# A two-layer streaming trunk: token-range tiles at the end of a mixer, FFN operands in two stages, an earlier first group of the second product, a bias table in three parts

## The chip, the cores and the metric

The kernel runs on one core of a Trainium2 chip. The metric is the device time of one execution in microseconds, as the median of several runs. The text calls the engines by their short names in the profile: PE is the tensor engine, PEld its weight loads, DVE is VectorE, ACT is ScalarE, POOL is GpSimd, and SP is the queue that issues nearly all transfers.

## The reference

One inference step of a trunk of two layers, on 1024 prompt tokens and 32 sample tokens (T = 1056), with 1024 features, in fp32. Layer 0 mixes by a gated linear recurrence, layer 1 by differential attention with a relative-position bias table. Each layer then ends in the same way, and this end is what the change touches:

```
x = x + rmsnorm(mixer(rmsnorm(x)), g_post)                  # sandwich norm
h = rmsnorm(x, g_in)
g, u = split(h @ w_ffn_in)                                  # 1024 -> 2 x 2816
g = causal depthwise conv of width 3 over tokens(g) + bias
f = (silu(g) * u) @ w_ffn_out                               # 2816 -> 1024
x = x + rmsnorm(f, g_post2)
x = x + sigmoid(x @ w_ple_gate) * (p @ w_ple)               # gated per-layer input
```

The bias of a head for a query and a key depends on their distance alone: `rel_bias[bucket(rel)]`, with 32 buckets and 8 heads.

## The kernel before

Features lie on partitions and tokens along the columns. An fp32 product is made of three matmuls of fp32r operands: each operand is split into a high part (a cast on ACT, L167 or L108) and a low part (a subtraction on DVE, L168 or L109), and `mm3` (L118 to L120) issues high x high, high x low and low x high. Tokens are cut in three groups GT: 384, 384 and 288 columns (t = 0, 1, 2).

`layer_end` is called once per layer. First `mixer_out` adds the second half of the mixer's output product: units (t, j) for three token groups and eight feature blocks j. In units of t = 0 the first half's result is added on DVE; in units of t = 1 and 2 an identity matmul adds it in PSUM (L292) and ACT copies it out (L293). `sumsq` squares on ACT (L200) and sums on POOL (L201) into `acc[t]`. `norm_m(t)` normalises, adds the residual (L308, L309), stores to `xm` and sums squares into `xacc[t]`; `norm_x(t)` (L318) writes the FFN's input y, eight tiles of 1060 columns. After the units, `ple` makes the per-layer input's product in eight steps, with norm_m(2) issued at step 0, norm_x(1) at step 1 and norm_x(2) at step 5. The matmul over `ones` in `rstd_ps` (L188) sums over partitions. PE's order there is the one written in the code.

The FFN's first product is done by seven products of half size instead of eight: the tokens are cut in two halves of HT = 528 columns and the features in two halves, `operands` makes the token-side operands b1 to b7 (differences of y, L398 to L401, then splits), `weights7` the weight-side ones, and `ffn_in` does 22 factors ft, one for each 128 of the 2816 hidden features. Each factor ends in the convolution and the gate (L499 to L504) and stores a row of 1056 columns to `hd`.

`ffn_out` makes the second product in groups of two or three hidden rows: each row is read from `hd`, split, and its weights `wfo` are loaded as a `piece` (L103, L108, L109). Group 0 is copied into f by ACT (L552), later groups are added on DVE (L554). The last group runs by token group; `post(t)` (L528, L529) norms the result, followed by the gates. Before group 3 of layer 0, `bias_table` loads the 0/1 table of buckets (`onehot`) in a raw slot, multiplies it with `rel_bias`, and stores the result to `bd`, which one transfer of 4608 KB then repeats over 128 partitions into `zd`.

A scheduler orders the instructions of each engine by program order, readiness and priority (`tc.high_priority()` raises it). Pools hand out tiles by tag: a tile waits until the slot's last user is done. `raw` has two slots of 1152 columns, shared by all weight loads. SP takes its transfers in order, and one that waits holds back those behind it.

Of the kernel before, what the change touches and what calls it, by code (L numbers as in the profile page):

```python
# [18 lines left out]
P = 128  # L19
# [19 lines left out]
HT = T // 2  # L39
NEG = -3.0e38  # L40
# [4 lines left out]
class Trunk:  # L45
# [228 lines left out]
    def mixer_out(self, l, wsrc, gpost, resid, fp):  # L274

        nc, tc, io = self.nc, self.tc, self.io
        with tc.tile_pool(name=self.nm("mo"), bufs=1, reuse_waits="tile") as mp:
            acc = [mp.tile([P, n], F32, tag=f"acc{t}", name=self.nm("acc")) for t, (_, n) in enumerate(GT)]
            xacc = self.new_acc()
            w = [self.piece(wsrc[1, jp]) for jp in range(4)]  # L280
            self.og_load(self.og, 4, 3, [2])
            ple = self.ple_load(l, mp)
            y = [fp.tile([P, T + 4], F32, tag="y", name=self.nm("y"), bufs=8) for _ in range(KD)]
            g_in = self.G(4 * l + 2)

            def unit(t, j):


                ps = self.half_unit(w, self.og, j, 4, t, t == 0)
                m = self.m[j][t].bitcast(F32)  # L290
                if t:
                    nc.tensor.matmul(ps, self.ident, m, start=False, stop=True)  # L292
                    nc.scalar.copy(m, ps)  # L293
                else:
                    nc.vector.tensor_tensor(m, ps, m, ADD)
                self.sumsq(acc[t], m, j == 0, mp)

            rm, rx = [None] * 3, [None] * 3

            def norm_m(t):  # L300
                self.ln_exp()
                rm[t] = self.rstd_ps(acc[t], D)
                t0, n = GT[t]
                for j in range(KD):
                    m = self.m[j][t].bitcast(F32)
                    x0 = mp.tile([P, 384], F32, tag="x0", name=self.nm("x0"), bufs=4)[:, :n]
                    nc.sync.dma_start(x0, resid[j][:, t0:t0 + n])
                    nc.vector.scalar_tensor_tensor(m, m, gpost[:, j:j + 1], rm[t], MUL, MUL)  # L308
                    nc.vector.tensor_tensor(m, m, x0, ADD)  # L309
                    nc.sync.dma_start(self.xm[j][:, t0:t0 + n], m)  # L310
                    self.sumsq(xacc[t], m, j == 0, mp)

            def norm_x(t):
                rx[t] = self.rstd_ps(xacc[t], D)
                t0, n = GT[t]
                for j in range(KD):
                    m = self.m[j][t].bitcast(F32)
                    nc.vector.scalar_tensor_tensor(y[j][:, t0:t0 + n], m, g_in[:, j:j + 1], rx[t], MUL, MUL)  # L318
# [17 lines left out]
        return y  # L336
# [12 lines left out]
    def ple(self, pool, ple, wpl):  # L349

        nc = self.nc
        for j in range(KD):
            js = slice(j * P, (j + 1) * P)
            pe = pool.tile([P, T], F32, tag="pe", name=self.nm("pe"), bufs=2)
            for t, (t0, n) in enumerate(GT):
# [3 lines left out]
                nc.scalar.copy(pe[:, t0:t0 + n], ps)  # L359
# [7 lines left out]
    def layer_end(self, l, wsrc, gpost, resid, last):  # L367

        tc = self.tc
        with self.phase("ff", 1, 2, m=4, r=1) as fp:  # L370
            y = self.mixer_out(l, wsrc, gpost, resid, fp)
            self.xp.release()
            op = self.right("op", 1)
            self.ffn_in(l, self.operands(y, op), fp)
            op.release()
            self.xp = self.right("xp", 16)
            with tc.tile_pool(name=self.nm("fo"), bufs=1, reuse_waits="tile") as f2:
                self.ffn_out(l, fp, f2, last)

    def operands(self, y, op):  # L380
# [3 lines left out]
        for p in (7, 5, 4, 1, 2, 3, 6):  # L384
            out[p] = [[op.tile([P, HT], F32R, tag=f"b{p}{k}{i}", name=self.nm(f"b{p}")) for i in range(2)]
                      for k in range(4)]

        def put(p, kh, hf):
            for k in range(4):
                self.split(b[kh][hf][k], *out[p][k])  # L390

        b = [[[y[4 * kh + k][:, HT * hf:HT * hf + HT] for k in range(4)] for hf in range(2)] for kh in range(2)]
        put(1, 0, 0)
        put(2, 1, 0)
        put(3, 1, 1)
        for k in range(4):
            b11, b12, b21, b22 = b[0][0][k], b[0][1][k], b[1][0][k], b[1][1][k]
            nc.vector.tensor_tensor(b11, b12, b11, SUB)  # L398
            nc.vector.tensor_tensor(b12, b22, b12, SUB)
            nc.vector.tensor_tensor(b22, b22, b11, SUB)  # L400
            nc.vector.tensor_tensor(b21, b21, b22, SUB)  # L401
        put(6, 1, 1)
        put(7, 0, 1)
        put(5, 0, 0)
        put(4, 1, 0)
        return out
# [26 lines left out]
    def ffn_in(self, l, b, fp):  # L433
# [6 lines left out]
        def row(tag="y", n=T + 4, bufs=8):  # L440
            return fp.tile([P, n], F32, tag=tag, name=self.nm(tag), bufs=bufs)

        for ft in range(NFF):
            a = self.weights7(l, ft)
# [14 lines left out]
            p1 = row("p1", HT, 1)  # L459
# [30 lines left out]
            prod(3, Z, more=True)  # L490
            n0, n1 = pieces
# [14 lines left out]
        nc.sync.dma_start(self.io["conv"][l], self.co[l])  # L506

    def ffn_out(self, l, fp, f2, last):
# [23 lines left out]
        groups = [[2 * i, 2 * i + 1] for i in range(8)] + [[16, 17, 18], [19, 20, 21]]  # L532
        for gi, grp in enumerate(groups):
            lastg = gi == len(groups) - 1
            hs, wos = [], []
            for ft in grp:
                raw = f2.tile([P, T], F32, tag="rh", name=self.nm("rh"), bufs=2) if gi else self.raw()[:, 0:T]
                nc.sync.dma_start(raw, self.hd[ft])
                h = [row()[:, 0:T].bitcast(F32R) for _ in range(2)]
                self.split(raw, *h)  # L540
                hs.append(h)
                wos.append(self.piece(io["wfo"][l, ft]))

            def out_unit(j, t):
# [8 lines left out]
                else:  # L553
                    nc.vector.tensor_tensor(f[j][t], ps, f[j][t], ADD)  # L554
                if lastg:
                    self.sumsq(acc[t], f[j][t], j == 0, f2)

            if gi == 3 and not last:
                self.bias_table()
# [457 lines left out]
    def bias_table(self):  # L1017
# [4 lines left out]
        nc.sync.dma_start(oh, io["onehot"])  # L1022
        nc.sync.dma_start(rb, io["rel_bias"])
        for i in range(3):
            ps = self.psm()[0:H, 0:384]
            nc.tensor.matmul(ps, rb, oh[:, i * 384:i * 384 + 384], start=True, stop=True)
            nc.vector.tensor_copy(bt[:, i * 384:i * 384 + 384], ps)
        nc.sync.dma_start(self.bd, bt)
# [294 lines left out]
```

## Time and profile before

| | |
|---|---|
| median of 3 runs | 3063.17 us (3062.08 to 3071.13) |
| the profiled execution, its own time | 3063.09 us |
| its span | 3061.1 us |
| PE busy | 2918.7 us (95%) |
| DVE busy | 1991.8 us (65%) |
| ACT busy | 1307.8 us (43%) |
| POOL busy | 278.5 us (9%) |
| mean granted PE clock | 0.979 |

Busy time is what an engine's instructions take; a share near 100% over a stretch says that the engine sets that stretch's length. The granted clock is PE's own, 1.00 being full speed.

### The profile page before, as it was taken

The numbers are of one execution on the slowest core, as the hardware profiler recorded it, in microseconds if no ns is written. First come the engines' busy times: TensorE is split into PE (matmuls) and PEld (weight loads), VectorE is DVE, ScalarE is ACT, GpSimd is POOL, SyncE is SP. The second block draws the span as 40 slices with busy tenths as digits, with TensorE's granted clock in tenths as the row PEclk, the third lists the DMA queues.
The fourth block names the chain that finished last, engine by engine and source line by source line (L and its number), as shares of the span: only waits on it lengthen the run. The fifth ranks groups of instructions, "written<-read, shape, count | busy, mean of one in ns | idle before, by whom it ended". The sixth has DMA issues, their size and how long they took to land.

```text
span 3061.1 us, 50577 instructions
## 1 busy us (share of the span) xinstructions
PE 2918.7 (95%) x20334; PEld 2800.4 (91%) x20334; DVE 1991.8 (65%) x3786; ACT 1307.8 (43%) x2347; POOL 278.5 (9%) x431
## 2 busy tenths in 40 slices
PE   7999999988999999898999999999889999999989
PEld 7998898978999999898988888989789999999989
DVE  7565555368777765666667575574787777657674
ACT  6444434564433333114445554465643433331151
POOL 0000000140000000002231111001400000000020
PEclk9999999998999999999999999999999999999999
DMA  3111111352222223422332232232512222242242
GB/s 130 38 46 40 45 53 40 104 180 68 72 82 79 79 83 120 158 93 93 124 119 72 85 91 80 90 101 79 181 56 81 74 79 82 81 136 84 84 143 71
DMA packets 104882, 275.32 MB, mean 90 GB/s; under 512 B 12192, under 2 KB 49056, under 8 KB 104648
## 3 DMA queue, kind: packets, MB, share of 16 engines
q1 hardware_dynamic: 102088, 263.71, 25.9%
q0 software_dynamic: 2560, 8.39, 1.3%
q8 instruction: 159, 2.61, 0.3%
q14 instruction: 75, 0.61, 0.1%
HBM read 196.53 MB, written 71.86 MB: 88 GB/s over the span
## 4 chain that ended last, share of the span: by engine, by line
PE 80%; DVE 8%; ACT 6%; DMA 2%; issue 2%; POOL 1%; SPq 0%; POOLq 0%; DVEq 0%; ACTq 0%
PE psm L120 14%; PE psm L119 14%; PE psm L118 13%; PE psd L118 10%; PE psd L119 10%; PE psd L120 10%; PE po L1167 1%; PE pss L1133 1%; PE psm L1159 1%; PE pss L1134 1%; DMA raw<-wfo 1%; POOL xacc L201 1%; ACT sq L200 1%; DVE ws L109 1%; ACT ws L108 1%
## 5 line engine op out<-in xcount | busy, mean ns | idle before, releaser
L118 PE MATMUL psd<-x,ws 128*128 128x384 f32 (+1 forms) x1512 | 519.4, 344 | 9.7 <-ACT x L622 8.8
L119 PE MATMUL psm<-b,ws 128*128 128x264 f32 x1760 | 504.2, 286 | 12.5 <-DVE b L168 12.5
L118 PE MATMUL psm<-b,ws 128*128 128x264 f32 x1760 | 504.0, 287 | 7.7 <-ACT b L167 7.7
L120 PE MATMUL psm<-b,ws 128*128 128x264 f32 x1760 | 504.0, 286 | 0.0
L119 PE MATMUL psd<-x,ws 128*128 128x384 f32 (+1 forms) x1512 | 496.5, 328 | 0.0
L120 PE MATMUL psd<-x,ws 128*128 128x384 f32 (+1 forms) x1512 | 492.0, 325 | 1.3 <-DVE ws L109 1.3
L118 PE MATMUL psm<-y,ws 128*128 128x384 f32 (+1 forms) x1056 | 348.6, 332 | 31.4 <-DVE f L554 14.5
L119 PE MATMUL psm<-y,ws 128*128 128x384 f32 (+1 forms) x1056 | 347.5, 329 | 4.9 <-DVE y L168 4.9
L119 PEld LDWEIGHTS psm<-b,ws 128*128 128x128 f32 x1760 | 335.0, 190 | 13.7 <-DVE b L168 13.7
L120 PE MATMUL psm<-y,ws 128*128 128x384 f32 (+1 forms) x1056 | 346.7, 329 | 0.6 <-DVE ws L109 0.6
L118 PEld LDWEIGHTS psm<-b,ws 128*128 128x128 f32 x1760 | 333.4, 190 | 8.6 <-ACT b L167 8.6
L120 PEld LDWEIGHTS psm<-b,ws 128*128 128x128 f32 x1760 | 334.6, 190 | 0.0
L167 ACT CAST ws<-raw 128x512 fp32r<-128x512 f32 x308 | 190.3, 621 | 325.6 <-DVE raw L429 101.1
L554 DVE TENSOR_TENSOR f<-psm,f 128x384 f32<-128x384 f32 (+1 forms) x432 | 220.6, 521 | 159.8 <-PE psm L120 158.7
L118 PEld LDWEIGHTS psd<-x,ws 128*128 128x128 f32 x1512 | 286.9, 190 | 23.7 <-ACT x L622 9.1
L119 PEld LDWEIGHTS psd<-x,ws 128*128 128x128 f32 x1512 | 287.3, 190 | 8.5 <-issue 0.9
L120 PEld LDWEIGHTS psd<-x,ws 128*128 128x128 f32 x1512 | 286.6, 190 | 6.9 <-issue 3.5
L168 DVE TENSOR_TENSOR ws<-raw,ws 128x512 fp32r<-128x512 f32 x308 | 208.7, 690 | 116.3 <-ACT ws L167 115.8
L109 DVE TENSOR_TENSOR ws<-raw,ws 128x1024 fp32r<-128x1024 f32 (+1 forms) x138 | 168.3, 1221 | 111.6 <-ACT ws L108 111.1
L118 PEld LDWEIGHTS psm<-y,ws 128*128 128x128 f32 x1056 | 203.3, 193 | 35.5 <-DVE f L554 15.1
L119 PEld LDWEIGHTS psm<-y,ws 128*128 128x128 f32 x1056 | 203.9, 193 | 7.6 <-DVE y L168 7.1
L120 PEld LDWEIGHTS psm<-y,ws 128*128 128x128 f32 x1056 | 203.1, 192 | 2.0 <-DVE ws L109 2.0
(295 smaller groups left out, 6083.9 us busy)
## 6 DMA issues: line engine op xcount, KB each, us to landing
raw<-wfi SPq DMA_DIRECT2D x88, 512.0 KB, 3.4
hd<-y SPq DMA_DIRECT2D x44, 528.0 KB, 2.7
raw<-wfo SPq DMA_DIRECT2D x44, 512.0 KB, 4.3
rh<-hd SPq DMA_DIRECT2D x40, 528.0 KB, 3.7
raw<-wia SPq DMA_DIRECT2D x30, 512.0 KB, 3.4
ped<-pe SPq DMA_DIRECT2D x16, 528.0 KB, 2.8
y<-ped SPq DMA_DIRECT2D x16, 528.0 KB, 5.1
raw<-wpg SPq DMA_DIRECT2D x16, 512.0 KB, 3.8
```

What stands on the lines that cost most here:

```text
L108: nc.scalar.copy(wh[:, w], raw[:, w])
L109: nc.vector.tensor_tensor(wl[:, w], raw[:, w], wh[:, w].bitcast(F32), SUB)
L118: mm(ps, wh, xh, start=start and i == 0, stop=False, skip_group_check=more)
L119: mm(ps, wh, xl, start=False, stop=False, skip_group_check=more)
L120: mm(ps, wl, xh, start=False, stop=stop and i == n - 1, skip_group_check=more)
L167: self.nc.scalar.copy(hi, src)
L168: self.nc.vector.tensor_tensor(lo, src, hi.bitcast(F32), SUB)
L200: nc.scalar.activation(sq, src, AF.Square)
L201: (eng or nc.gpsimd).tensor_tensor(acc, acc, sq, ADD)
L554: nc.vector.tensor_tensor(f[j][t], ps, f[j][t], ADD)
L1133: mm(ps[:, :pad], qs[c][:, P * i:P * i + P], kh[c][:, k0:k0 + pad], start=True, stop=False)
L1134: mm(ps[:, :pad], qs[c][:, P * i:P * i + P], kl[c][:, k0:k0 + pad], start=False, stop=True)
```

## The change

The change has five parts. All but the last are done in both layers.

1. `mixer_out` keeps y in three tiles by token range (528, 240 and 288 columns) in a pool of its own. Units of t = 1 are added on DVE instead of PE and ACT; only t = 2 keeps the identity matmul, and its result goes straight to y's third tile. The squares get high priority and those of `xacc` a tag of their own. norm_m(1) is issued after unit (2, 1) instead of (2, 2).
2. `operands` becomes a generator with two stages. The first, begun after norm_x(1) and before norm_x(2), covers b1, b2 and the first 240 columns of the second half; the second does the other 288 columns and the rest. The first factor's weights are split before the second stage.
3. `out_operands`, new, loads and splits a group's rows and weights. For group 0 it is called in the last factor of `ffn_in`, behind product 3.
4. The adds into f and the last squares in `ffn_out` get high priority.
5. `bias_table` works in three parts of 384 columns, in tiles of the tags sg and x0 instead of raw slots.

```diff
@@ mixer_out
-                ps = self.half_unit(w, self.og, j, 4, t, t == 0)
+                ps = self.half_unit(w, self.og, j, 4, t, t < 2)
                 m = self.m[j][t].bitcast(F32)
-                if t:
+                if t == 2:
                     nc.tensor.matmul(ps, self.ident, m, start=False, stop=True)
+                    m = y[j][2]
                     nc.scalar.copy(m, ps)
                 else:
                     nc.vector.tensor_tensor(m, ps, m, ADD)
-                self.sumsq(acc[t], m, j == 0, mp)
+                with tc.high_priority():
+                    self.sumsq(acc[t], m, j == 0, mp)
...
-                    self.sumsq(xacc[t], m, j == 0, mp)
+                    self.sumsq(xacc[t], m, j == 0, mp, tag="sqx")
...
-                    if (t, j) == (2, 2):
+                    if (t, j) == (2, 1):
                         norm_m(1)
                 for j in self.ple(mp, *ple):
                     if j == 0:
                         norm_m(2)
                     if j == 1:
                         norm_x(1)
+                        self.xp.release()
+                        out = self.operands(y)
+                        next(out)
                     if j == 5:
-                        norm_x(2)
+                        with tc.high_priority():
+                            norm_x(2)
@@ operands
+        cut = YT[1][1]
+        parts = slice(0, cut), slice(cut, HT)
...
+        def sums(i):
+            put(3, 1, 1, i)
+            for k in range(4):
+                b11, b12, b22 = b(0, 0, k, i), b(0, 1, k, i), b(1, 1, k, i)
+                nc.vector.tensor_tensor(b11, b12, b11, SUB)
+                nc.vector.tensor_tensor(b12, b22, b12, SUB)
+                nc.vector.tensor_tensor(b22, b22, b11, SUB)
+            put(6, 1, 1, i)
...
         put(1, 0, 0)
         put(2, 1, 0)
+        sums(0)
+        sum4(0)
+        yield
+        sums(1)
+        self.opb = self.right("opb", 1)
+        alloc(self.opb, (7, 5, 4))
+        for i in range(2):
+            put(7, 0, 1, i)
         put(5, 0, 0)
+        sum4(1)
         put(4, 1, 0)
@@ ffn_in
             prod(3, Z, more=True)
+            if ft == NFF - 1:
+                ready = self.out_operands(l, OUT[0], row, lambda: self.raw()[:, 0:T])
@@ new
+    def out_operands(self, l, grp, row, raw):
+
+        hs, wos = [], []
+        for ft in grp:
+            r = raw()
+            self.nc.sync.dma_start(r, self.hd[ft])
+            hs.append([row()[:, 0:T].bitcast(F32R) for _ in range(2)])
+            self.split(r, *hs[-1])
+            wos.append(self.piece(self.io["wfo"][l, ft]))
+        return hs, wos
@@ ffn_out
-                    nc.vector.tensor_tensor(f[j][t], ps, f[j][t], ADD)
+                    with tc.high_priority():
+                        nc.vector.tensor_tensor(f[j][t], ps, f[j][t], ADD)
@@ bias_table
-        oh, bt = self.raw()[0:32, 0:1152], self.raw()[0:H, 0:1152]
...
         for i in range(3):
+            w = slice(i * 384, i * 384 + 384)
+            oh, bt = (pool.tile([P, 384], F32, tag=tag, name=self.nm(tag), bufs=2) for tag in ("sg", "x0"))
+            nc.sync.dma_start(oh[0:32], io["onehot"][:, w])
             ps = self.psm()[0:H, 0:384]
```

Three places show how the engines' orders change. The first is POOL's order at the end of layer 0's mixer, before. `acc_5407` is the sum of group 2, `xacc_5409` and `xacc_5410` are those of the normed groups 1 and 2:

```order
L201 TENSOR_TENSOR xacc_5409<-xacc_5409,sq_5930 128x384
L201 TENSOR_TENSOR xacc_5409<-xacc_5409,sq_5938 128x384
L201 TENSOR_TENSOR xacc_5409<-xacc_5409,sq_5946 128x384
L201 TENSOR_TENSOR xacc_5409<-xacc_5409,sq_5954 128x384
L201 TENSOR_TENSOR acc_5407<-acc_5407,sq_5972 128x288
L201 TENSOR_TENSOR acc_5407<-acc_5407,sq_5990 128x288
L201 TENSOR_TENSOR acc_5407<-acc_5407,sq_6008 128x288
L201 TENSOR_TENSOR acc_5407<-acc_5407,sq_6026 128x288
L201 TENSOR_TENSOR acc_5407<-acc_5407,sq_6044 128x288
L201 TENSOR_TENSOR xacc_5410<-xacc_5410,sq_6089 128x288
```

And POOL's order now, where `acc_5415` is the sum of group 2 and `xacc_5417` that of the normed group 1 (its line has become L203):

```order
L203 TENSOR_TENSOR xacc_5417<-xacc_5417,sq_5904 128x384
L203 TENSOR_TENSOR xacc_5417<-xacc_5417,sq_5912 128x384
L203 TENSOR_TENSOR acc_5415<-acc_5415,sq_6006 128x288
L203 TENSOR_TENSOR xacc_5417<-xacc_5417,sq_5920 128x384
L203 TENSOR_TENSOR xacc_5417<-xacc_5417,sq_5928 128x384
L203 TENSOR_TENSOR acc_5415<-acc_5415,sq_6024 128x288
L203 TENSOR_TENSOR xacc_5417<-xacc_5417,sq_5936 128x384
L203 TENSOR_TENSOR acc_5415<-acc_5415,sq_6042 128x288
L203 TENSOR_TENSOR xacc_5417<-xacc_5417,sq_5944 128x384
L203 TENSOR_TENSOR xacc_5417<-xacc_5417,sq_5952 128x384
L203 TENSOR_TENSOR acc_5415<-acc_5415,sq_6060 128x288
L203 TENSOR_TENSOR xacc_5418<-xacc_5418,sq_6105 128x288
```

The adds into the sum of group 2, which stood in one block behind those of the normed group 1, now alternate with them.

The second place is ACT's order at the last factor of layer 0, before. `y_11641` and `y_11653` are the high parts of group 0's hidden rows, `ws_11658` is the second wfo piece, L499 and L502 belong to the last factor's gate:

```order
L478 COPY y_11450<-psm_11423 128x264
L478 COPY y_11450<-psm_11424 128x264
L499 ACTIVATE y_11620<-y_11450,ffc 128x1058
L167 CAST y_11641<-raw_11639 128x1056
L167 CAST y_11653<-raw_11651 128x1056
L167 CAST y_11881<-rh_11879 128x1056
L502 ACTIVATE y_11620<-y_11620 128x1058
L108 CAST ws_11658<-raw_11657 128x1024
L167 CAST y_11893<-rh_11891 128x1056
L108 CAST ws_11886<-raw_11885 128x1024
```

The same place now (`y_11688`, `y_11700` and `ws_11705`; the gate's lines have become L551 and L554):

```order
L528 COPY y_11521<-psm_11494 128x264
L528 COPY y_11521<-psm_11495 128x264
L169 CAST y_11688<-raw_11686 128x1056
L169 CAST y_11700<-raw_11698 128x1056
L110 CAST ws_11705<-raw_11704 128x1024
L110 CAST ws_11958<-raw_11957 128x1024
L609 COPY f_11742<-psm_11735 128x384
L551 ACTIVATE y_11715<-y_11521,ffc 128x1058
L609 COPY f_11751<-psm_11744 128x384
```

The casts of group 0 now stand before the last factor's gate, and its first copies (L609, before L552) stand before it too.

The third place is DVE's order in the tail of layer 0's second product, before, where post(0) begins:

```order
L554 TENSOR_TENSOR f_11760<-psm_13964,f_11760 128x384
L528 SCALAR_TENSOR_TENSOR f_11670<-f_11670,gc,psd_13896 128x384
L528 SCALAR_TENSOR_TENSOR f_11697<-f_11697,gc,psd_13896 128x384
L529 TENSOR_TENSOR f_11670<-f_11670,x_1822_13900 128x384
L529 TENSOR_TENSOR f_11697<-f_11697,x_1825_13908 128x384
L528 SCALAR_TENSOR_TENSOR f_11724<-f_11724,gc,psd_13896 128x384
L168 TENSOR_TENSOR x_1824_13905<-f_11670,x_1823_13904 128x384
```

Twenty-two rows of post(0) stand there between two adds of L554. The same place now (L554 has become L612, L528 has become L592, L529 L593 and L168 L170):

```order
L612 TENSOR_TENSOR f_11832<-psm_14044,f_11832 128x384
L592 SCALAR_TENSOR_TENSOR f_11742<-f_11742,gc,psd_13976 128x384
L612 TENSOR_TENSOR f_11859<-psm_14058,f_11859 128x384
L593 TENSOR_TENSOR f_11742<-f_11742,x_1850_13980 128x384
L592 SCALAR_TENSOR_TENSOR f_11769<-f_11769,gc,psd_13976 128x384
L612 TENSOR_TENSOR f_11886<-psm_14072,f_11886 128x384
L170 TENSOR_TENSOR x_1852_13985<-f_11742,x_1851_13984 128x384
L612 TENSOR_TENSOR f_11913<-psm_14086,f_11913 128x384
L593 TENSOR_TENSOR f_11769<-f_11769,x_1853_13988 128x384
L592 SCALAR_TENSOR_TENSOR f_11796<-f_11796,gc,psd_13976 128x384
L612 TENSOR_TENSOR f_11940<-psm_14100,f_11940 128x384
```

An add of the last group now stands between nearly every two rows of post(0).

## Rows read from the trace of the kernel before

**Rows 1.** The page's head: span and instructions.

```profile
span 3061.1 us, 50577 instructions
```

**Rows 2.** Busy by 50 us stretch: length, then PE, PEld, DVE, ACT, POOL, clock.

```profile
...
750.00:800.00 50.00, 50.00 (x412) 50.00 (x412) 35.45 (x65) 20.04 (x33) 1.96 (x8) 1.00 0.22 76
```

**Rows 3.** The tensor engine's waits: us in total, times, longest.

```profile
...
PE psm L188 <- POOL acc L201: 19.2, 2, 9.6
PE psm L118 <- DVE f L554: 18.1, 4, 7.4
PE psm L119 <- DVE b L168: 12.5, 4, 6.0
PE psm L118 <- ACT ws L108: 10.9, 3, 7.7
...
PE psm L118 <- ACT b L167: 7.7, 4, 2.2
PE psm L118 <- ACT y L167: 6.0, 2, 3.0
```

**Rows 4.** Timeline of PE: start, us, line, operation, [idle before <-releaser].

```profile
661.84 1.33 PE L188 MATMUL psm<-acc,ones 128*128 128x288 f32 x2 [9.60 <-POOL acc L201]
...
680.72 0.65 PE L188 MATMUL psm<-xacc,ones 128*128 128x288 f32 x2
...
707.52 0.59 PE L119 MATMUL psm<-b,ws 128*128 128x264 f32 x1 [5.95 <-DVE b L168]
```

**Rows 5.** Stretches around waits: length, PE busy (count), granted clock, DMA.

```profile
...
655.00:668.00 13.00, 6.16 (x24) 0.61 0.40 134
698.00:716.00 18.00, 9.80 (x51) 0.62 0.00 1
1156.00:1168.00 12.00, 8.32 (x25) 0.57 0.79 238
1260.00:1275.00 15.00, 7.25 (x32) 0.66 0.68 249
1428.00:1440.00 12.00, 7.25 (x37) 0.72 0.22 66
```

**Rows 6.** Timeline of POOL, the same columns.

```profile
...
656.19 4.49 POOL L201 TENSOR_TENSOR acc<-acc,sq 128x288 f32<-128x288 f32 x4
...
673.10 1.67 POOL L201 TENSOR_TENSOR xacc<-xacc,sq 128x288 f32<-128x288 f32 x2 [0.99 <-ACT sq L200]
```

**Rows 7.** Timeline of DVE, end of the mixer and operands.

```profile
...
664.14 0.94 DVE L308 SCALAR_TENSOR_TENSOR x<-x,gc,psm 128x288 f32<-128x288 f32 x2 [0.60 <-ACT psm L190]
665.00 0.82 DVE L309 TENSOR_TENSOR x<-x,x 128x288 f32<-128x288 f32 x2
665.73 0.93 DVE L308 SCALAR_TENSOR_TENSOR x<-x,gc,psm 128x288 f32<-128x288 f32 x2
...
682.34 3.49 DVE L318 SCALAR_TENSOR_TENSOR y<-x,gc,psm 128x288 f32<-128x288 f32 x8 [6.40 <-ACT psm L190]
687.41 2.11 DVE L168 TENSOR_TENSOR ws<-raw,ws 128x512 fp32r<-128x512 f32 x3 [1.59 <-ACT ws L167]
689.44 7.50 DVE L168 TENSOR_TENSOR b<-y,b 128x528 fp32r<-128x528 f32 x12
696.86 1.32 DVE L398 TENSOR_TENSOR y<-y 128x528 f32<-128x528 f32 x2
```

**Rows 8.** The chain that ended last, near the bias table: start, us.

```profile
...
1239.82 27.67 DMA raw<-wfo
```

**Rows 9.** DMA issues: KB each, median us from issue to landing.

```profile
...
S<-state SPq DMA_DIRECT2D x8, 64.0 KB, 1.9
...
raw<-onehot SPq DMA_DIRECT2D x1, 144.0 KB, 2.5
```

**Rows 10.** Timeline of DVE, tail of the second product.

```profile
...
1421.04 1.14 DVE L528 SCALAR_TENSOR_TENSOR f<-f,gc,psd 128x384 f32<-128x384 f32 x2 [1.11 <-ACT psd L190]
...
1432.14 0.55 DVE L554 TENSOR_TENSOR f<-psm,f 128x384 f32<-128x384 f32 x1
```

More of the change, by code (lines that the diff above doesn't have):

```diff
@@ L39 @@
 HT = T // 2
+YT = [(0, HT), (HT, GT[2][0] - HT), GT[2]]
+OUT = [[2 * i, 2 * i + 1] for i in range(8)] + [[16, 17, 18], [19, 20, 21]]
 NEG = -3.0e38
@@ L370, in layer_end @@
         with self.phase("ff", 1, 2, m=4, r=1) as fp:
[L371 to L380, printed above, removed]
+            with tc.tile_pool(name=self.nm("yp"), bufs=1, reuse_waits="tile") as yp:
+                self.p1 = fp.tile([P, HT], F32, tag="p1", name=self.nm("p1"))
+                for i in range(4):
+                    fp.tile([P, 1024], F32R, tag=f"x{i}", name=self.nm("ws"), bufs=1)
+                b = self.mixer_out(l, wsrc, gpost, resid, yp)
+                w = self.weights7(l, 0)
+                b = next(b)
@@ L382, in operands @@
+            with tc.tile_pool(name=self.nm("rp"), bufs=1, reuse_waits="tile") as rp:
+                ready = self.ffn_in(l, w, b, fp, rp)
+                self.opb.release()
+                self.opa.release()
+                self.xp = self.right("xp", 16)
+                with tc.tile_pool(name=self.nm("fo"), bufs=1, reuse_waits="tile") as f2:
+                    self.ffn_out(l, rp, f2, ready, last)
+    def operands(self, y):
         nc = self.nc
         out = {}
-        for p in (7, 5, 4, 1, 2, 3, 6):
-            out[p] = [[op.tile([P, HT], F32R, tag=f"b{p}{k}{i}", name=self.nm(f"b{p}")) for i in range(2)]
-                      for k in range(4)]
@@ L388, in put, with alloc @@
-        def put(p, kh, hf):
-            for k in range(4):
-                self.split(b[kh][hf][k], *out[p][k])
-        b = [[[y[4 * kh + k][:, HT * hf:HT * hf + HT] for k in range(4)] for hf in range(2)] for kh in range(2)]
+        def alloc(op, ps):
+            for p in ps:
+                out[p] = [[op.tile([P, HT], F32R, tag=f"b{p}{k}{i}", name=self.nm(f"b{p}")) for i in range(2)]
+                          for k in range(4)]
+        cut = YT[1][1]
+        parts = slice(0, cut), slice(cut, HT)
@@ new lines, in b, with put @@
+        def b(kh, hf, k, i):
+            return y[4 * kh + k][1 + i] if hf else y[4 * kh + k][0][:, parts[i]]
+        def put(p, kh, hf, i=None):
+            for k in range(4):
+                c = slice(0, HT) if i is None else parts[i]
+                self.split(y[4 * kh + k][0] if i is None else b(kh, hf, k, i), *[o[:, c] for o in out[p][k]])
+        def sums(i):
[6 more added lines that the diff above has]
+            put(6, 1, 1, i)
@@ L393, in operands, with sum4 @@
+        def sum4(i):
+            for k in range(4):
+                nc.vector.tensor_tensor(b(1, 0, k, i), b(1, 0, k, i), b(1, 1, k, i), SUB)
+        self.opa = self.right("opa", 1)
+        alloc(self.opa, (1, 3, 2, 6))
         put(1, 0, 0)
         put(2, 1, 0)
[L395 to L401, printed above, removed]
@@ L458, in ffn_in @@
             prod(1, X)
-            p1 = row("p1", HT, 1)
+            p1 = fp.tile([P, HT], F32, tag="p1", name=self.nm("p1"))
             gp = row()
@@ L530, in post @@
                 self.store_x(t, j, y, None, f2, new=True)
[L532 to L542, printed above, removed]
+        for gi, grp in enumerate(OUT):
+            lastg = gi == len(OUT) - 1
+            hs, wos = ready if gi == 0 else self.out_operands(l, grp, row, lambda: f2.tile(
+                [P, T], F32, tag="rh", name=self.nm("rh"), bufs=2))
             def out_unit(j, t):
```

54 lines of the change are left out of this document (32 added, 22 removed).

## The prediction

> **What bounds the kernel now.** I began with the span [rows 1], since everything below is counted against it: the profiled execution took 3063.09 us, 2.0 more than its span, and lies 0.1 under the median of the runs shown, so the sum can be made against 3063.1. Then I cut the span into stretches of 50 us. In the steady part of the FFN the tensor engine fills its stretch completely while VectorE is busy for 35 of the 50 us [rows 2]; there only fewer matmuls would help, and the change leaves that loop's order as it was. Time can be won only where the tensor engine stands still, so the third view is its table of waits [rows 3]: nearly all its waits of several us belong to the ends of the layers, and most come once per layer. [...]
>
> **Parts 1 and 2, from the mixer's end to the FFN's first factor, once per layer.** Now the tensor engine idles for 9.60 us before the matmul that sums the squares of token group 2 [rows 4]. The releaser is POOL: it first does all squares of the normed group 1, and then four adds for group 2 in one block of 4.49 us from 656.19 on, and a last one [rows 6]. Two things change. The t=1 units lose their identity matmul, and the second norm is issued one unit earlier; against that, three of these units now wait for a psd bank, because their adds stand behind norm_m(0) on VectorE. I take an estimate of 3 us earlier for norm_m(1); none is the low end. And the squares get buffers and priorities of their own, so that POOL's order alternates between the two sums and one add is left behind the last instead of the block: some 4.2 us more. The sum is then complete 7.2 us earlier, near 654.6. The VectorE work of norm_m(2) starts 2.3 us behind that matmul now (664.14 against 661.84 [rows 4, 7]), which would be 656.9; but the weight splits of the FFN's first factor stand ahead of it in the new order. Between 656.9 and an unchanged 664.1 I take 660.5.
>
> What follows is norm_x(2), which starts at 682.34 on VectorE after 6.40 us of idling [rows 7]. POOL had its squares ready at about 674.8 [rows 6]; the matmul that sums them came only at 680.72 [rows 4], since it stands in the tensor engine's order behind five of eight ple steps. By the tensor engine's way this matmul moves from 680.72 by 7.2, and by about 2 of the 2.4 us that the low clock costs there (6.16 us at 0.61 [rows 5]), to 671.5. By VectorE's way it moves to 660.5 plus the 10.6 from 664.14 to 674.8, 671.1. The two agree, so norm_x(2) starts near 673.9 with the same 1.6 us to its first instruction and some 0.8 for what is queued: 8.4 us earlier.
>
> From there VectorE is the pace. Its 28 splits at 0.62 each (7.50 for twelve) and 16 differences at 0.62 (1.32 for two, overlapping) [rows 7] make 27 us that stand between norm_x(2) and the last operand; the tensor engine waits on them for 6.2 us per layer, most of it before 707.52, and on ScalarE's casts for 3.9 [rows 3, 4]. The change takes none of this work away. Its order has one split ahead of norm_x(2) and seven uncut ones right behind it, and it cuts the operands of the second half in 240 and 288 columns. That makes 28 more VectorE instructions per layer. Two adds of 288 columns start 0.365 us apart (665.00 to 665.73), one of 528 takes 0.62 [rows 7]; so a piece of 240 is about 0.315, and a pair costs 0.06 more than the whole: 1.7 us per layer. The split ahead of norm_x(2) takes 0.6 out of the row, and the 1.59 us of idling before 687.41 [rows 7] is filled by splits that are ready: 2.2 less, nearly the same. So the FFN's first factor ends about as much earlier as norm_x(2): **8.5 us per layer, 17 in all**. The bounds are nothing (VectorE takes back all that it got) and 23.4 per layer: the three idle terms, 9.6 + 6.2 + 3.9, and 3.7 of low clock (9.80 us at 0.62 [rows 5]).
>
> [...]
>
> **Part 3, the second product's first group, once per layer.** Behind the last factor the tensor engine waits 3.0 us for ScalarE's casts of the group's hidden rows, and about 1.6 for the cast of the second wfo piece (10.9 less the 7.7 of another place, for two layers) [rows 3]. The clock takes 8.32 times 0.43, so 3.6 more [rows 5]. Issued after product 3, the loads leave SP's queue ahead of the last hidden row's store, and in ScalarE's new order the two casts and the wfo cast stand ahead of that factor's gate activations. The rest of the gate then lies beside the group's matmuls; only the last group needs its result. I take 8 of the 8.2, **16 in all**; the low bound is 6, if the last transfer still lands a little late.
>
> **Part 5, the bias table, layer 0 only.** The chain that ended last contains 27.67 us for two wfo pieces issued at 1239.82 [rows 8], directly behind the 4608 KB broadcast zd on SP's queue. The tensor engine pays 7.7 of idling for it [rows 3] and 7.25 times 0.34, so 2.5, of clock [rows 5]. Without the two raw slots the pieces are loaded ahead of zd, which now stands before the loads of a later group. New is a wait: the third part's tile is freed only by the first part's matmul, and the third matmul stands in the tensor engine's order ahead of the group's first. Its 48 KB lie below the 1.9 us of a 64 KB load and the 2.5 of the old table [rows 9]; with the issue I take 2.4. The part gives 10.2 - 2.4, **7.8**; bounds 5 and 10.
>
> **Part 4, the tail of the second product, once per layer.** VectorE runs post(0) from 1421.04 to 1432.14 while finished psum banks wait for their add [rows 10]; the tensor engine waits on these adds for 9.05 us per layer (18.1 for both) [rows 3], and loses 7.25 times 0.28, 2.0, to the clock [rows 5]. With priority each add stands ahead of the next norm instruction, so these waits go. But post(0) is then done some 7 us later, and the splits of post(1) and of the gate's weights behind it; the third gate's weights come, by the new order, about 3 us after they are wanted. I take 8 of 11 per layer, **16 in all**; bounds 5 and 11.
>
> **The sum** is 17 + 16 + 7.8 + 16 = 56.8 us, so 3063.1 becomes 3006. Moves of the steady factors, attention and the first recurrent layer: none, and I cost them at nothing, since their order on every engine is as before.
>
> **The rivals.** (a) The mixer's parts give nothing, because VectorE's pieces and its weight splits eat the 8.4 us. For it speaks that VectorE is the pace in that stretch; against it, that it idles for 6.40 us there. Time: 3006 + 17 = 3023. (b) They give nearly all, because the first operands are enough to feed products 1, 2 and 6 while the rest is made: 2 x (23.4 - 8.5) less, 2976. Against it stand 27 us of splits after norm_x(2), unless ScalarE and VectorE run further ahead than I think. (c) The broadcast zd, not the raw slots, was what delayed the wfo pieces, and a later group pays the same 10.2: 3016. (d) The other side: the hidden rows and operands lie in new pools, and a row's release could come later in every factor. The price is per factor: 42 steady factors of both layers turn the gain over from 56.8 / 42 = 1.35 us each; at 2 us the time is 3090. Against it: the tensor engine is at 50.00 of 50 with 15 us to spare on VectorE [rows 2]; a row's store, not its place, would have to be late. (e) The change doesn't do what it says: the waits move to the next instruction, say the gates and group 1, and the time stays within 0.3%, 3054 to 3072.
>
> **How the numbers follow.** My sum 0.60, (a) 0.14, (b) 0.10, (c) 0.08, (d) 0.04, (e) 0.04. A change of 0.3%, 9 us, is about what a measurement of this kernel tells from none. So faster 0.92, same 0.04, slower 0.04. With every low bound but the mixer's own chosen value the sum is 12 + 5 + 10 + 17 = 44, 3019; with the mixer at half of that 3028. Toward (b), the mixer at 18.5 per layer gives 2986. The range 2986 to 3028 holds my sum, (a) and (c), and leaves (b), (d) and (e) outside, together 0.18.
>
> **What would show it.** The wait of the sum on POOL falls from 9.6 to some 4 us; norm_x(2) starts on VectorE about 8 us closer to the end of the mixer's last unit, and the tensor engine's first long wait of the FFN is on VectorE's splits, with some 3 us for products 5 or 7. Behind the last factor there is no wait over 1 us and the clock stays at 1.00. Three bias matmuls show a gap of 2 to 2.5 us before the third, and no wfo wait follows. In the tail the wait on the f adds is gone, and one of 3 to 4 us stands before a gate. I am wrong if the steady stretches are no longer full, if norm_m(2) starts no earlier than now, or if the tail's wait on VectorE comes back in full at the gates.

## The result, and the profile after

The changed kernel took 3024.86 us in the median of four runs (3021.87 to 3029.06), the kernel before 3065.73 on the same chip; the ratio is 0.9866 [0.9844, 0.9889]. A repeat on another chip gave 3023.02 us and 0.9868 [0.9851, 0.9884]. That is 40.9 us faster, inside the range and 72% of the 56.8 us forecast. The profiled execution took 3029.06 us by its own time, its span 3027.3.

The first view is the tensor engine's table of waits for the changed kernel (what it waited for: us in total, times, longest). The helpers' lines have moved by two or three: L201 is now L203, L168 is L170.

```profile
PE psd L120 <- ACT b L169: 17.0, 2, 8.5
...
PE psd L120 <- DVE x L304: 7.2, 2, 3.6
PE psm L122 <- DVE ws L111: 6.4, 3, 3.7
PE psm L181 <- POOL xacc L203: 6.4, 1, 6.4
...
PE psm L190 <- POOL acc L203: 3.7, 2, 2.2
...
PE psm L121 <- DVE b L170: 2.8, 2, 1.4
...
PE psm L1086 <- DMA sg<-onehot: 1.3, 1, 1.3
PE psm L120 <- DVE f L612: 0.3, 1, 0.3
```

Against [rows 3]: the sum's wait on POOL fell from 19.2 to 3.7, the wait on the f adds from 18.1 to 0.3, and those on the hidden rows' casts and the wfo cast are gone. But 17.0 us on ScalarE's casts of b are new, twice 8.5. They stand at the FFN's start, where most of the missing gain is found below. Behind the last factor and in the steady part (us, then PE, PEld, DVE, ACT and POOL busy with counts, granted clock, DMA share, GB/s):

```profile
750.00:800.00 50.00, 50.00 (x412) 50.00 (x411) 35.42 (x65) 19.95 (x33) 1.97 (x8) 1.00 0.21 75
1150.00:1200.00 50.00, 50.00 (x322) 50.00 (x321) 29.03 (x42) 21.59 (x36) 0.30 (x2) 1.00 0.50 164
```

Both stretches are full at clock 1.00. So rival (d), a later release in every factor, is out, and the second product's first group starts without a wait.

### The profile page after: what moved, and what is told of

It reads as the page before. It is cut to its first block, busy times and chain, and to the rows that moved or that the text cites. A ratio compares the mean times of both kernels' runs of the same rounds, so it can differ in the third digit from the quotient of the medians.

```text
span 3027.3 us, 50591 instructions
## 1 busy us (share of the span) xinstructions
PE 2908.7 (96%) x20302; PEld 2796.0 (92%) x20302; DVE 2002.4 (66%) x3874; ACT 1298.9 (43%) x2355; POOL 285.1 (9%) x431
## 4 chain that ended last, share of the span: by engine, by line
PE 82%; DVE 10%; ACT 5%; issue 2%; DMA 1%; POOL 1%; SPq 0%; DVEq 0%; ACTq 0%; POOLq 0%
PE psm L122 14%; PE psm L120 14%; PE psm L121 14%; PE psd L120 10%; PE psd L121 10%; PE psd L122 10%; PE po L1227 1%; DVE b L170 1%; PE pss L1193 1%; PE psm L1219 1%; PE pss L1194 1%; DVE ws L111 1%; DVE x L170 1%; PE po L1229 1%; ACT ws L110 1%
## 5 line engine op out<-in xcount | busy, mean ns | idle before, releaser
L121 PE MATMUL psm<-y,ws 128*128 128x384 f32 (+1 forms) x1056 | 343.4, 326 | 5.6 <-DVE y L170 5.6
L120 PE MATMUL psm<-y,ws 128*128 128x384 f32 (+1 forms) x1056 | 344.9, 327 | 0.4 <-DVE f L612 0.3
L122 PE MATMUL psm<-y,ws 128*128 128x384 f32 (+1 forms) x1056 | 342.1, 325 | 0.0
L612 DVE TENSOR_TENSOR f<-psm,f 128x384 f32<-128x384 f32 (+1 forms) x432 | 221.1, 522 | 156.6 <-PE psm L122 155.5
L170 DVE TENSOR_TENSOR ws<-raw,ws 128x512 fp32r<-128x512 f32 x308 | 211.4, 698 | 114.2 <-ACT ws L169 113.8
L120 PE MATMUL psd<-b,ws 128*128 128x264 f32 x704 | 200.1, 285 | 17.0 <-ACT b L169 17.0
L121 PEld LDWEIGHTS psm<-y,ws 128*128 128x128 f32 x1056 | 200.6, 190 | 7.8 <-DVE y L170 7.0
L120 PEld LDWEIGHTS psm<-y,ws 128*128 128x128 f32 x1056 | 200.2, 190 | 3.1 <-ACT ws L110 1.3
```

The source lines that it names most:

```text
L120: mm(ps, wh, xh, start=start and i == 0, stop=False, skip_group_check=more)
L121: mm(ps, wh, xl, start=False, stop=False, skip_group_check=more)
L122: mm(ps, wl, xh, start=False, stop=stop and i == n - 1, skip_group_check=more)
L170: self.nc.vector.tensor_tensor(lo, src, hi.bitcast(F32), SUB)
```

## The experiments

**Parts 1 and 2 alone (x_mixer).** The kernel before with the hunks of `mixer_out`, `ple`, `layer_end` and `operands`; group 0 of the second product is still read in `ffn_out`:

```diff
+                b = self.mixer_out(l, wsrc, gpost, resid, yp)
+                w = self.weights7(l, 0)
+                b = next(b)
...
+                self.ffn_in(l, w, b, fp, rp)
```

> Parts 1 and 2 alone on the kernel before. Theory A (the mixer's parts give nothing, because what VectorE gets earlier is lost again before the first factor ends): the time is that of before within 3 us, and the last matmul of the first factor ends where it ended before, within 1 us, although the first product starts some 4.7 us earlier. Theory B (the prediction's sum: 8.5 us per layer): 17 us less than before. Theory C (the parts give something alone, and lose it only beside the others): between 5 and 17 us less.

3063.59 us against 3065.43, 0.9993 [0.9985, 1.0001]: about 2 us, and the interval does not exclude that it is none. That is theory A.

**Part 3 alone (x_ready).**

```diff
             prod(3, Z, more=True)
+            if ft == NFF - 1:
+                ready = self.out_operands(l, OUT[0], row, lambda: self.raw()[:, 0:T])
```

> Part 3 alone on the kernel before. All theories: the waits on the casts of group 0 and on its second wfo piece go, and the low clock behind them, 8 to 9 us per layer, 16 to 18 us less than before. If only the place of the wait moves, less than 6.

3046.29 us against 3065.43, 0.9936 [0.9923, 0.9949]: 19 us. In this run's trace the 6.0 us on the hidden rows' casts [rows 3] are gone, and the 10.9 on ScalarE's casts of ws have become 7.6, which is the bias table's place.

**Part 4 alone (x_tail).**

```diff
-                    nc.vector.tensor_tensor(f[j][t], ps, f[j][t], ADD)
+                    with tc.high_priority():
+                        nc.vector.tensor_tensor(f[j][t], ps, f[j][t], ADD)
                 if lastg:
-                    self.sumsq(acc[t], f[j][t], j == 0, f2)
+                    with tc.high_priority():
+                        self.sumsq(acc[t], f[j][t], j == 0, f2)
```

> Part 4 alone on the kernel before. The wait on the f adds goes (11 us per layer with the clock), and a wait of 2 to 4 us for a gate's weights comes, with a dip of the clock. Theory A: 12 to 13 us less than before in all, layer 0 giving 3 to 4 and layer 1 9. Theory B (the prediction's 8 per layer): 16 us less.

3052.08 us against 3065.43, 0.9952 [0.9936, 0.9968]: 13 us by the medians, 15 by the ratio.

**Part 5 alone (x_bias).** The hunk of `bias_table`, as in the diff above:

```diff
+            oh, bt = (pool.tile([P, 384], F32, tag=tag, name=self.nm(tag), bufs=2) for tag in ("sg", "x0"))
+            nc.sync.dma_start(oh[0:32], io["onehot"][:, w])
```

> Part 5 alone on the kernel before. The wait of 7.75 us for wfo goes; a wait for the third part's table of 1 to 2.5 us comes. Theory A (the new wait also lowers the clock for about 7 us, which costs another 3.4): 5 to 6 us less than before. Theory B (the prediction: 10.2 less 2.4): 8 us less. If the broadcast zd delays a later group by as much: no change.

3064.0 us against 3065.43, 0.9989 [0.9979, 0.9999]: 1.4 us by the medians, 3.4 by the ratio. The four ratios multiplied give 0.9870; the whole change gave 0.9866 and 0.9868. The parts add up, so each part's miss can be looked for in that part alone.

**Is VectorE the pace at the FFN's start? (a_nodiff)** The changed kernel without its 32 differences per layer:

```diff
-                nc.vector.tensor_tensor(b11, b12, b11, SUB)
-                nc.vector.tensor_tensor(b12, b22, b12, SUB)
-                nc.vector.tensor_tensor(b22, b22, b11, SUB)
...
-                nc.vector.tensor_tensor(b(1, 0, k, i), b(1, 0, k, i), b(1, 1, k, i), SUB)
+            return
```

> The changed kernel without the 32 differences of the operands in each layer (the operands are then splits of y as it is; this leaves out that part of the computation). They take some 11 us of VectorE per layer. Theory A (VectorE's work behind norm_x(2) is the pace of the first factor): the wait of 8.5 us for product 5 or 6 falls below 2, the low clock behind it goes, and the first factor ends 8 to 12 us earlier per layer, 16 to 24 us less in all. Theory B (the tensor engine's order or ScalarE sets the pace): less than 6 us in all.

3002.99 us, 0.9795 [0.9781, 0.9808], so 22 us less than the changed kernel. The differences' own price, by the spacings read further down, is 16 x 0.32 + 16 x 0.37 = 11.0 us per layer, 22.1 for both. The gain is as large as that price, so VectorE's work there stands on the path. It is not the price alone: the wait of 8.5 us goes too (0.43 and 1.77 us are left), and behind it the clock is higher (0.92 from 694.00 to 714.30, where the changed kernel has 0.77 from 699.60 to 725.90). In layer 0 the first factor's last adds come 13.1 us earlier, counted as further down.

**Shorten the way to norm_x(2) (a_sum4).** The root of norm_m(2) gets priority, and norm_x(2) comes one ple step earlier:

```diff
-                        norm_m(2)
+                        norm_m(2, True)
...
-                    if j == 5:
+                    if j == 4:
                         with tc.high_priority():
```

> The changed kernel with two edits in the mixer's end: the root of group 2's sum (norm_m(2)) gets high priority on ScalarE, where it waited behind copies and weight casts, and norm_x(2) comes after ple step 4 instead of 5. Theory A (the earlier sum was lost on ScalarE, and VectorE then sets the pace): norm_m(2) starts on VectorE within 3 us of the sum's matmul instead of 6, norm_x(2) some 3 us earlier, the first factor ends 3 to 5 us earlier per layer, 6 to 10 us less than the changed kernel. Theory B (the pace comes later, from the operands' order and the low clock after the long wait): norm_x(2) moves, but the first factor ends within 1 us of where it did.

3033.32 us, 0.9894 [0.988, 0.9908]: no gain, 8 us more than the changed kernel by the medians, with overlapping intervals. VectorE's timeline in this run (start, us, what, and in brackets the idling before it with its releaser):

```profile
666.71 0.94 DVE L319 SCALAR_TENSOR_TENSOR y<-y,gc,psm 128x288 f32<-128x288 f32 x2
...
680.66 3.49 DVE L332 SCALAR_TENSOR_TENSOR y<-y,gc,psm 128x288 f32<-128x288 f32 x8 [2.26 <-ACT psm L192]
...
689.33 1.33 DVE L170 TENSOR_TENSOR b<-y,b 128x528 fp32r<-128x528 f32 x2 [4.16 <-ACT b L169]
```

The first edit missed its aim: the sum's matmul started at 661.32 here, and norm_m(2) (666.71) followed it 5.4 us later, hardly sooner than the 6.0 of the changed kernel. So what ScalarE's order costs there was not tested. The second edit worked: norm_x(2) followed the sum 19.3 us later instead of 22.6. But VectorE then idled 4.16 us for ScalarE's first casts of b: the wait moved one block on. Counted as further down, the first product started 3.5 us later than in the changed kernel and the first factor's last adds 2.6 later; neither theory had that.

**Feed the tensor engine in another order (a_order).** The first factor's products as 1, 2, 5, 3, 6, 7, 4 instead of 1, 2, 6, 7, 5, 4, 3, operands made in the same order, product 5 copied out by ScalarE:

```diff
+                    prod(5, Z)
+                    u = row()
+                    with tc.high_priority():
+                        for s, n in enumerate(pieces):
+                            nc.scalar.copy(u[:, HT + n.start:HT + n.stop], Z[s])
+                    prod(3, Z, more=True)
+                    prod(6, Y)
```

> The changed kernel with another order of the first factor: operands are made in the order b1, b2, b5, b3, b6, b7, b4, and the tensor engine does products 1, 2, 5, 3, 6, 7, 4 (product 5 is copied out by ScalarE before product 3 is added to it). The work is the same but for those two copies. Theory A (VectorE's work is the pace, and the order of its results leaves the tensor engine idle for 8.5 us in one piece, with low clock after it): the idle time falls into pieces of 2 to 4 us, the low clock shrinks, and the first factor ends within 3 to 5 us of VectorE's last split instead of 11, 14 to 20 us less than the changed kernel in all. Theory B (the sum of VectorE's work alone counts, the tensor engine catches up in any order): less than 5 us.

3029.16 us, 0.9886 [0.9871, 0.99], no better than the changed kernel. Theory A missed; the number of theory B came, but not its reason, for the tensor engine did not catch up. The tensor engine's and ScalarE's timelines:

```profile
712.93 0.59 PE L120 MATMUL psd<-b,ws 128*128 128x264 f32 x1 [15.46 <-ACT y L533]
```

```profile
708.90 2.23 ACT L169 CAST b<-y 128x528 fp32r<-128x528 f32 x4 [5.48 <-DVE y L436]
...
712.50 0.38 ACT L533 COPY y<-psd 128x264 f32<-128x264 f32 x1 [1.08 <-DVE b L170]
```

Product 5's copies stood behind the casts of b4 on ScalarE, and those waited for VectorE's last differences. Here a product was held for 15.46 us by the engine that was to empty its bank.

**The bias table without its third wait (a_bias).** All three parts of `onehot` are loaded at once, and each product goes back into its own tile:

```diff
+        ohs = [pool.tile([P, 384], F32, tag=tag, name=self.nm(tag), bufs=2) for tag in ("sg", "sg", "x0")]
+        for oh, w in zip(ohs, ws):
             nc.sync.dma_start(oh[0:32], io["onehot"][:, w])
+        for oh, w in zip(ohs, ws):
             ps = self.psm()[0:H, 0:384]
             nc.tensor.matmul(ps, rb, oh[0:32], start=True, stop=True)
-            nc.vector.tensor_copy(bt[0:H], ps)
+            nc.vector.tensor_copy(oh[0:H], ps)
```

> The changed kernel with all three parts of the onehot table loaded at once: three tiles, and each product goes back into its part's own tile. Theory A (the 1.3 us wait for the third part, and about 7 us of low clock that follow it, are what eats the bias part's gain): no wait between the bias matmuls and no low clock there, 4 to 5 us less than the changed kernel. Theory B (the broadcast zd holds up a later group's weights, wherever it stands): a wait of several us for wfo comes back, no gain.

3018.29 us (3017.28 to 3023.29), 0.9848 [0.9835, 0.9862]: the best version by its median, though its interval still overlaps that of the changed kernel. With a_order added (a_both):

> The new order of the first factor and the onehot table loaded at once, together. If the two are independent, their gains add: 19 to 26 us less than the changed kernel by theory A, 5 to 10 by theory B.

3026.35 us, 0.9872 [0.9858, 0.9887]: 8 us above a_bias by the medians, the intervals just overlapping. Both theories missed; a_order gives nothing here either.

**The gate's weights earlier (a_gate).**

```diff
+            with tc.high_priority():
+                wg.update({j: self.piece(io["wpg"][l, j]) for j in range(NA)})
```

> The changed kernel with high priority for the first five gate weights' loads and splits. Theory A (the gates wait 3.7 and 2.3 us for a weight split that stands behind post(1) on VectorE): these waits go, 5 us in layer 0 and 2 to 3 in layer 1, if the end of layer 0 doesn't take them back at its last sum of squares: 3 to 8 us less than the changed kernel. Theory B (the tail is bound by VectorE's sum of work): another wait of the same size comes behind it, no gain.

3028.62 us, 0.9878 [0.9864, 0.9891]: no gain. The tensor engine's waits of this run from 1380 to 1560:

```profile
PE psm L181 <- POOL xacc L203: 6.4, 1, 6.4
PE psm L120 <- ACT x L169: 2.6, 1, 2.6
...
PE psm L122 <- DVE ws L111: 0.4, 1, 0.4
```

The 3.7 us for the gate's weights are gone (the 0.4 stands before 1390, ahead of the gates), and a wait of 2.6 for the cast of x came in their place. That is theory B.

**Parts 3 and 4 with the better bias table, on the mixer of before (x_three).** The hunks of x_ready, x_tail and a_bias on the kernel before, so that only the mixer's parts differ from a_bias:

```diff
+                ready = self.out_operands(l, OUT[0], row, lambda: self.raw()[:, 0:T])
...
+        ohs = [pool.tile([P, 384], F32, tag=tag, name=self.nm(tag), bufs=2) for tag in ("sg", "sg", "x0")]
```

> Parts 3 and 4 on the kernel before, with its own mixer and operands, and the bias table in three parts that are all loaded at once. Theory A (the mixer's parts give nothing, also beside the others): 0.985 of the kernel before within 0.002, as the changed kernel with that table. Theory B (the mixer's parts give what was forecast when the other waits are gone): 0.988 to 0.991, 10 us or more slower than that kernel.

3026.57 us (3021.46 to 3032.12), 0.9869 [0.9847, 0.9891]. It lies 8 us above a_bias by the medians, and the intervals overlap: inconclusive, the mixer's parts being worth between nothing and 8 us here. The same kernel run again (after_again):

> The changed kernel once more, on the chip of the next two: 0.985 to 0.989 of the kernel before.

It gave the repeat named at the top, in agreement with the first.

## Why the prediction was right or wrong

**Parts 1 and 2: 17 us forecast, 2 measured alone.** This is nearly the whole miss. The time is that of rival (a), 3023, which had 0.14; its reason, VectorE's pieces and weight splits, is only a small part of what the traces show. I count from the end of the tensor engine's last wait for the mixer's weights (the mark: 591.35 before, 593.15 after; the executions differ by 1.8 us before any changed code). The stretch from there to the end of the FFN's first product falls in two at the first matmul on b, first before, then after:

```profile
591.35:689.30 97.95, 84.25 (x475) 78.82 (x475) 65.68 (x104) 61.60 (x124) 45.69 (x42) 0.95 0.55 186
689.30:1154.90 465.60, 456.37 (x3696) 455.06 (x3696) 341.57 (x600) 185.24 (x304) 21.25 (x86) 0.98 0.23 77
```

```profile
593.15:684.60 91.45, 81.74 (x458) 78.33 (x459) 70.95 (x119) 58.16 (x116) 46.16 (x42) 0.94 0.59 195
684.60:1154.90 470.30, 456.99 (x3698) 455.53 (x3697) 347.05 (x631) 188.41 (x319) 23.47 (x86) 0.98 0.23 78
```

The FFN starts 6.5 us earlier and then takes 4.7 longer. In x_mixer, where these parts stand alone, its first product starts 5.2 us earlier against the mark, and the first factor's last adds 0.1. The steps can be followed in the changed kernel. POOL's, the tensor engine's, ScalarE's and VectorE's timelines:

```profile
654.18 2.85 POOL L203 TENSOR_TENSOR xacc<-xacc,sq 128x384 f32<-128x384 f32 x2
657.00 1.24 POOL L203 TENSOR_TENSOR acc<-acc,sq 128x288 f32<-128x288 f32 x1
```

```profile
658.29 1.33 PE L190 MATMUL psm<-acc,ones 128*128 128x288 f32 x2 [2.18 <-POOL acc L203]
...
678.34 0.65 PE L190 MATMUL psm<-xacc,ones 128*128 128x288 f32 x2
```

```profile
659.35 0.39 ACT L378 COPY pe<-psd 128x288 f32<-128x288 f32 x1
659.76 1.28 ACT L126 ACT_TABLE_LOAD   x1
661.58 0.48 ACT L378 COPY pe<-psd 128x384 f32<-128x384 f32 x1 [0.54 <-PE psd L122]
661.95 0.48 ACT L191 ACTIVATE psm<-psm,eps 128x288 f32<-128x288 f32 x1
662.35 0.62 ACT L169 CAST ws<-raw 128x512 fp32r<-128x512 f32 x1
663.50 0.48 ACT L378 COPY pe<-psd 128x384 f32<-128x384 f32 x1 [0.53 <-PE psd L122]
663.87 0.41 ACT L192 ACTIVATE psm<-psm 128x288 f32<-128x288 f32 x1
```

```profile
664.31 0.94 DVE L318 SCALAR_TENSOR_TENSOR y<-y,gc,psm 128x288 f32<-128x288 f32 x2 [0.62 <-ACT psm L192]
...
680.93 3.49 DVE L331 SCALAR_TENSOR_TENSOR y<-y,gc,psm 128x288 f32<-128x288 f32 x8
684.33 5.69 DVE L170 TENSOR_TENSOR b<-y,b 128x528 fp32r<-128x528 f32 x11
...
693.77 1.35 DVE L170 TENSOR_TENSOR b<-y,b 128x240 fp32r<-128x240 f32 x4
...
709.52 1.56 DVE L439 TENSOR_TENSOR y<-y,y 128x288 f32<-128x288 f32 x4
711.00 2.56 DVE L170 TENSOR_TENSOR b<-y,b 128x528 fp32r<-128x528 f32 x4
...
714.07 0.77 DVE L505 TENSOR_TENSOR y<-psm,p 128x264 f32<-128x264 f32 x2
```

Against the mark norm_m(1) came 2.8 us earlier where 3 was forecast, and POOL left one add behind the last square, as said. The step that failed first is "some 4.2 us more". The sum came 3.6 us earlier by the times of the profile, 5.4 against the mark; 7.2 was forecast. So the new order gave 2.6: POOL has no idle time left from 643.93 to 658.24, and its own adds now set the sum.

Between the sum and the two steps of its root ScalarE did a table load, copies of the ple product, which the change gives priority, and a cast of weights. From the sum to norm_m(2) it now takes 6.0 us instead of 2.3 [rows 4, 7]. The forecast had 5.9 there (654.6 to 660.5), but for weight splits on VectorE; it was ScalarE's order, so that this size came out is luck. norm_m(2) starts 1.6 us earlier against the mark and no earlier by the times of the profile (664.31, before 664.14), which was one of the signs of being wrong.

The step that cost most is "By the tensor engine's way this matmul moves from 680.72 by 7.2, and by about 2 of the 2.4 us that the low clock costs there". It moved by 4.2 against the mark, to 678.34. From the one sum's matmul to the other, before and after:

```profile
661.84:680.72 18.88, 17.75 (x95) 16.96 (x96) 13.49 (x27) 11.30 (x28) 6.03 (x7) 0.90 0.67 237
```

```profile
658.29:678.34 20.05, 18.61 (x94) 17.83 (x95) 16.11 (x38) 13.70 (x31) 6.02 (x7) 0.86 0.70 250
```

The mean clock fell from 0.90 to 0.86 instead of rising, and the stretch took 1.2 us longer instead of 2 less. So norm_x(2) came 3.2 us earlier against the mark, not 8.4.

The last failed step is "So the FFN's first factor ends about as much earlier as norm_x(2)". VectorE's last split of b (in the changed kernel the four from 711.00 on) and the factor's last adds, before and after:

```profile
718.53 0.70 DVE L168 TENSOR_TENSOR b<-y,b 128x528 fp32r<-128x528 f32 x1
...
725.03 0.49 DVE L455 TENSOR_TENSOR y<-psd,y 128x232 f32<-128x232 f32 x2
```

```profile
725.43 0.49 DVE L505 TENSOR_TENSOR y<-psd,y 128x232 f32<-128x232 f32 x2
```

The last adds start 1.4 us earlier against the mark, 2.8 if layer 1 is taken alike, which is near the 2 measured. The operands were not late: the last split ends at 713.6 against 719.2, 7.5 us earlier against the mark. What was won goes behind it, where 11.9 us instead of 5.8 pass up to the last adds.

The price of the cut held: pieces of 240 and 288 columns follow each other by 0.32 and 0.37 us (1.35 for four, 1.56 for four, less the first one's own 0.40 and 0.45), whole ones by 0.62, so 28 pairs cost 1.9 us per layer, where 1.7 was forecast; by these spacings an extra piece costs 0.07 us.

The tensor engine can't use the early start: it does products 1 and 2 and then waits 8.49 us, up to 699.56, for b's casts, which follow VectorE's differences; the first add that empties a bank of product 6 stands at 714.07, behind the last split, and the products after it come late. Before, five adds stood ahead of the last split. That VectorE's work is on the path here is shown by a_nodiff. That the adds' place costs the last few us is read from the trace and no run shows it, since a_order moved the wait to ScalarE; nor is it told apart from the low clock behind the 8.49 us.

Of the signs named ahead, the fall of the sum's wait (9.6 to 2.2), the full steady stretches and the wait before a gate came. norm_x(2) did not come 8 us closer, and the FFN's first long wait was on ScalarE's casts, 8.49 us, not on VectorE's splits.

**Part 3: 16 forecast, 19 measured.** The mechanism is as written: the waits are gone, and the clock is 1.00 behind the last factor. The size was a little low; where the other 3 us lie is not shown.

**Part 4: 16 forecast, 13 to 15 measured.** The wait on the adds went as said, 18.1 to 0.3 [rows 3]. "I take 8 of 11" was a little high. The waits from 1390 on in layer 0's end, before and with part 4 alone:

```profile
PE psm L118 <- DVE f L554: 8.8, 2, 7.1
PE psm L179 <- ACT sg L574: 4.3, 1, 4.3
...
PE psm L179 <- POOL xacc L201: 1.7, 1, 1.7
```

```profile
PE psm L179 <- POOL xacc L201: 6.4, 1, 6.4
...
PE psm L120 <- DVE ws L109: 1.8, 1, 1.8
PE psm L179 <- ACT sg L576: 1.1, 1, 1.1
```

What post(0) gets later is not only the gate's weights, which I had named, but also the last sum of squares on POOL, 4.7 us more. In the whole change the gate's wait is 3.7, as the 3 to 4 us forecast; a_gate shows that taking it away alone brings the next one.

**Part 5: 7.8 forecast, 1.4 to 3.4 measured alone.** The removal was sized rightly: from the table's first matmul to the tail's first sum the kernel before takes 183.49 us and a_bias 173.30, the 10.2 of the prediction. Rival (c), that zd delays a later group by the same, is out. The term that was wrong is the 2.4 for the new wait; it idles for only 1.33, but that is not all that it costs. By stretches, the changed kernel's first profiled execution and a_bias, and then the repeat's (with its third bias matmul from the tensor engine's timeline):

```profile
1224.55:1228.69 4.14, 2.81 (x7) 0.38 (x7) 3.92 (x6) 3.51 (x4) 0.00 (x0) 0.83 0.34 83
1228.69:1236.00 7.31, 7.31 (x30) 7.31 (x30) 4.36 (x7) 0.00 (x0) 0.00 (x0) 0.63 0.82 248
1224.55:1405.65 181.10, 176.21 (x1043) 171.98 (x1043) 113.63 (x187) 33.70 (x39) 7.55 (x8) 0.97 0.35 115
```

```profile
1223.80:1397.10 173.30, 170.85 (x1043) 168.40 (x1043) 112.70 (x187) 33.74 (x39) 7.57 (x8) 1.00 0.36 119
1225.80:1233.00 7.20, 7.20 (x45) 7.15 (x45) 6.80 (x12) 1.54 (x2) 0.00 (x0) 1.00 0.55 174
```

```profile
1223.55 0.80 PE L1086 MATMUL psm<-sg,rb 32*8 32x384 f32 x2 [1.26 <-DMA sg<-onehot]
...
1224.40:1231.70 7.30, 7.30 (x45) 7.30 (x46) 6.34 (x11) 0.00 (x0) 0.00 (x0) 1.00 0.91 285
```

In the first, the clock behind the short wait is 0.63 for 7.31 us and 30 matmuls fit in; without the wait 45 fit in 7.20. The forecast's clock terms are the busy time of a stretch of [rows 5] times what its mean clock lacks of 1.00; that is the author's estimate, and no run shows one of them alone. Reckoned in that way the loss here is 2.7 us (7.31 x 0.37), and by the counts some 2.5 (7.31 less 30/45 of 7.20). But the wait does not always do this: in the repeat it is 1.26 us, the clock behind it stays at 1.00, and 45 matmuls fit in 7.30. In the seven traced executions that have the wait the clock there was 0.63, 0.62 (x_bias), 0.77 (a_gate), 0.77 (a_sum4) and three times 1.00 (the repeat, a_order, a_nodiff); in the seven that do not have it, 1.00. What decides it is not shown. With a second dip around 1390 (0.83 over 10 us), whose cause is not shown either, the whole stretch took 181.10 us in the first execution and 176.70 in the repeat's. So the part gave 2.4 and 6.8 us, and against a_bias the new wait and what went with it cost 7.8 and 3.4 us, not 2.4.

Measured less forecast, by the ratios of the parts alone: the mixer's parts -15 us, part 3 +4, part 5 -4, part 4 -1, together the miss of 16. That the time lies inside the range does not speak for the sum: the range was drawn wide enough to hold (a), and the misses of parts 3 and 5 cancel.

## What to carry to other kernels

When a wait is taken away, follow what it releases through the order of each engine up to the point where time is counted: here POOL's own adds, the tensor engine's order with its low clock, and the place of VectorE's adds each took back a part of the gain. Operands that were ready 7.5 us earlier let the block end only 1.4 earlier, while leaving out 22.1 us of VectorE's work in the two blocks gave 22. Parts that touch different places can be measured alone and added up (here 0.9870 for the four parts against 0.9866 for the whole), and that says faster than the whole profile which one failed.

## What was not expected of the hardware

A wait of some 1.3 us among three small matmuls was followed by about 7 us at 0.62 to 0.77 of the full clock in four traced executions, and by full clock in three; in the prediction such a loss went only with waits of several us. And two executions of one kernel differ by more than the parts that were to be weighed: the changed kernel's two profiled executions took 3029.06 and 3015.68 us, at mean clocks of 0.983 and 0.986. Of these 13.4 us, 2.5 lie before any changed code and 4.4 between the bias table's first matmul and the tail's first sum. Differences of some 5 us between versions are settled only by intervals over several runs.
